# A hybrid decoder step on one Trainium2 core: layer-norm scaling and weight subtracts from GpSimd to VectorE, second buffers for loaded rows, squares out of PSUM, first combinations in product order

## The chip, the cores and the metric

The kernel runs on one core of one Trainium2 chip. It is written with a tile framework: tiles come from pools with a number of buffers, and a scheduler puts the instructions into one queue for each engine. The metric is the device time of one execution in microseconds (us); lower is better. Before the change three runs gave 3063.54, 3064.39 and 3066.76 us, median 3064.39.

The engines are named as in the profile: PE is TensorE (matmuls), PEld its weight loads, DVE is VectorE, ACT is ScalarE, POOL is GpSimd, SP is SyncE, which here issues most of the DMAs. Each engine works off its own queue in order; an instruction that waits holds up all that stand behind it.

## The reference

One step of a two-layer decoder on 1024 prompt rows and 64 sample rows of width 1024, in float32. Layer 0 mixes with a gated short convolution, layer 1 with differential attention (prompt rows causally, sample rows against a paged cache of 2048 keys). After each mixer comes a SwiGLU feed-forward net of width 2816, and after each of the four parts a layer norm over the residual sum.

```python
# layer 0:
gb, gc, h = split(x @ w_in, 3);  u = gc * h
conv = w_taps[0]*u_pad[:, 0:S] + w_taps[1]*u_pad[:, 1:S+1] + w_taps[2]*u_pad[:, 2:S+2]
m = (gb * conv) @ w_out
# layer 1: q, k, v = rope(split(x @ w_qkv, 3)); a = softmax(q1 k1) - lam * softmax(q2 k2)
#          m = (rmsnorm(a @ v) * subln_g * (1 - lam_init)) @ w_attn_out
# both layers:
x = layernorm(ALPHA * x + m) * ln_mix_g + ln_mix_b
x = layernorm(ALPHA * x + (silu(x @ w_gate) * (x @ w_up)) @ w_down) * ln_ffn_g + ln_ffn_b
```

Beside the two `x` (1024 and 64 rows) the outputs are the convolution's last rows and the new keys and values.

## The kernel before

**Precision.** A float32 operand is split in two parts: `hi` is a rounded copy made by ScalarE, `lo` the rest, made by a subtraction (`split_to`, lines 78 to 80). A product is then three matmuls, hi x hi, hi x lo and lo x hi (`passes`). So each loaded tile costs one cast on ScalarE (L79) and one subtract (L80 on VectorE, or L91 on GpSimd in two halves).

**Stages, in order of time.** Loading of `x` and the first combinations (0 to 47 us); the convolution's in-product (to 292); its out-product (to 457); FFN0 in (to 955) and out (to 1304); attention (1304 to 2061); its out-product (2073 to 2238); FFN1 in (to 2717) and out (to the end).

**In-products** (`InPhase`) are Strassen products with seven instead of eight block products. The seven combinations of the blocks of `x` are held split in `xh` and `xl` (`Combos`); those of the weights, `ws`, are made step by step from loaded `raw` tiles by `Weights.make`. The names B11, B21, B22, X1 to X4 are the combinations; the first products need them in the order B11, B21, X3, X2, X1, X4, B22. PE's order is written out by hand there. `load_x` makes the first set of combinations: for two halves `ch` of the columns and two halves `kk` of the inner index it loads four blocks, and makes all seven combinations of one `kk` before it goes to the next.

**Out-products** (`OutPhase`) take row tiles of 128 in three groups (`PAIRED` = (0,4,1), (5,2,6), (3,7) for conv and attention, `PLAIN` = (0,1,2), (3,4,5), (6,7) for the FFNs). For each group they run over all steps `f` (8 in conv and attention, 22 in the FFNs). A step needs a weight tile (`raw`, split to `whi` and `wlo`) and the rows (`hr` from DRAM, split to `hh` and `hl`), and in the first group the sample rows `hs`. `prep` issues them three steps ahead. `whi` and `wlo` come from a pool of seven buffers (`wsp`, tag "w"), `hh` and `hl` from two, `hr` and `hs` from one. Two tiles of a group use 6 matmuls each in a step. At the end of a group `ln_prompt` does the layer norm of each tile: residual sum on VectorE (L416), square with row sum on ScalarE (L421, whose unused full output goes over the product's PSUM tile), the rest on VectorE and GpSimd. Turning the rows into the next stage's operand (transposes on PE, casts and subtracts) goes into the following group's steps, as the list `side`. In the FFN stages the residual rows `x` are first multiplied with the gain and added to the bias of the layer norm before (L374, L375 on GpSimd), since the rows were stored without these.

**What sets the order.** Outside blocks marked `manual_schedule` the framework's scheduler sets the order of each engine's queue, from dependencies, buffers and its own idea of durations. So a buffer more, or work on another engine, can change the order of instructions that aren't touched. In PE's case the in-products and the attention are in the written order.

Lines the text speaks of: L79 (casts), L80 and L91 (subtracts), L222 (a weight combination), L260 (in-products), L345 (out-products), L385 (sample rows' product), L416 to L431 (layer norm), L835 (sample rows' q, k, v in attention), L1048 (prompt rows' q, k, v), L1158 to L1176 (the last normalisation in attention and its transposes).

## Time and profile before

| | |
|---|---|
| three runs | 3063.54, 3064.39, 3066.76 us |
| the profiled execution | 3066.03 us, span 3064.3 us |
| PE busy | 2787.6 us, 91% of the span |
| VectorE busy | 1490.7 us, 49% |
| ScalarE busy | 1095.6 us, 36% |
| GpSimd busy | 506.7 us, 17% |
| granted PE clock, mean | 0.969 |

The profile is of one execution. Busy times of matmuls overlap a little, since they are pipelined. A row of groups reads: line, engine, operation, output <- inputs (partitions x elements), count, busy us, mean ns of one, idle of that engine just before and what ended it. A wait is put down to what came last by the profile. The granted clock is PE's, 1.00 at full speed.

### The profile page before, as it was taken

The page shows a single profiled execution, that of the slowest core. Times are in us where ns is not written, and L with a number is a line of the kernel's source. Part 1 is how long each engine was busy: PE and PEld are TensorE (multiplying, and loading weights), DVE is VectorE, ACT ScalarE, POOL GpSimd, SP SyncE. Part 2 cuts the span into 40 slices and gives each one's busy share as a digit, 9 for nine tenths or more (in the row PEclk, how much of TensorE's full clock was granted, in tenths as well). Part 3 has the DMA queues.
Part 4 walks back from the last instruction along what each step waited for, and adds up shares of the span by engine and source line. Part 5 has one row for each costly group of instructions (what it writes and reads, how often), then busy time and mean ns, then how long its engine had stood idle before and what let it go on. Part 6 is the DMA issues. An engine that isn't in the chain of part 4 may idle for free. (4 is left out here: it accounts for less than half of the span.)

```text
span 3064.3 us, 51378 instructions
## 1 busy us (share of the span) xinstructions
PE 2787.6 (91%) x20468; PEld 2372.9 (77%) x20468; DVE 1490.7 (49%) x2527; ACT 1095.6 (36%) x2080; POOL 506.7 (17%) x638
## 2 busy tenths in 40 slices
PE   5999869999998988689999999988789999989886
PEld 5999559999995666479888666655579999976664
DVE  6675355445443365322222566662565454543553
ACT  4322364333331233211221556552553333322332
POOL 1001550000002031011111232344410000020310
PEclk8999999999999999989999999998899999999999
DMA  3222542222224455366787888735422222244653
GB/s 109 69 73 70 179 155 78 79 78 71 81 79 142 135 180 185 127 222 217 247 282 263 292 301 305 262 105 163 154 88 77 78 71 85 77 134 141 200 180 110
DMA packets 193442, 455.45 MB, mean 149 GB/s; under 512 B 43025, under 2 KB 84514, under 8 KB 193202
## 3 DMA queue, kind: packets, MB, share of 16 engines
q1 hardware_dynamic: 180322, 408.05, 40.6%
q0 software_dynamic: 12160, 42.81, 4.1%
q8 instruction: 160, 2.62, 0.4%
q10 hardware_dynamic: 720, 1.31, 0.1%
q14 instruction: 80, 0.66, 0.1%
HBM read 387.66 MB, written 64.43 MB: 148 GB/s over the span
## 5 line engine op out<-in xcount | busy, mean ns | idle before, releaser
L260 PE MATMUL pin<-xh,ws 128*128 128x272 f32 x6272 | 1204.6, 290 | 46.2 <-ACT gc L284 12.4
L260 PEld LDWEIGHTS pin<-xh,ws 128*128 128x128 f32 x6272 | 1001.2, 190 | 52.8 <-ACT gc L284 12.9
L260 PE MATMUL pin<-xl,ws 128*128 128x272 f32 x3136 | 913.1, 291 | 8.0 <-DVE xl L80 8.0
L260 PEld LDWEIGHTS pin<-xl,ws 128*128 128x128 f32 x3136 | 594.7, 190 | 9.4 <-DVE xl L80 9.1
L345 PE MATMUL pout<-whi,hh 128*128 128x512 f32 x960 | 408.1, 426 | 109.6 <-ACT hh L79 106.0
L345 PE MATMUL pout<-whi,hl 128*128 128x512 f32 x960 | 389.6, 417 | 30.9 <-DVE hl L80 30.6
L345 PE MATMUL pout<-wlo,hh 128*128 128x512 f32 x960 | 392.9, 410 | 7.1 <-DVE wlo L80 7.1
L80 DVE TENSOR_TENSOR wlo<-raw,whi 128x1024 fp32r<-128x1024 f32 x156 | 211.5, 1357 | 337.5 <-ACT whi L79 163.1
L345 PEld LDWEIGHTS pout<-whi,hh 128*128 128x128 f32 x960 | 189.8, 198 | 216.7 <-ACT hh L79 156.6
L79 ACT CAST whi<-raw 128x1024 fp32r<-128x1024 f32 x156 | 163.5, 1048 | 405.5 <-DMA raw<-wfo 197.3
L79 ACT CAST ws<-s 128x512 fp32r<-128x512 f32 x224 | 139.0, 622 | 442.9 <-PE pin L260 415.2
L80 DVE TENSOR_TENSOR ws<-s,ws 128x512 fp32r<-128x512 f32 x212 | 146.3, 690 | 262.8 <-ACT ws L79 262.8
L345 PEld LDWEIGHTS pout<-whi,hl 128*128 128x128 f32 x960 | 190.8, 199 | 96.2 <-DVE hl L80 55.0
L345 PEld LDWEIGHTS pout<-wlo,hh 128*128 128x128 f32 x960 | 190.8, 199 | 51.7 <-DVE wlo L80 9.2
L1048 PE MATMUL psqkv<-whi,xTh 128*128 128x256 f32 x768 | 223.1, 290 | 5.6 <-ACT pout L421 5.6
L80 DVE TENSOR_TENSOR hl<-hr,hh 128x384 fp32r<-128x384 f32 (+1 forms) x180 | 125.5, 697 | 205.6 <-ACT hh L79 187.9
L1048 PE MATMUL psqkv<-wlo,xTh 128*128 128x256 f32 x768 | 214.8, 280 | 0.0
L1048 PE MATMUL psqkv<-whi,xTl 128*128 128x256 f32 x768 | 214.5, 279 | 0.0
L374 POOL TENSOR_TENSOR x<-x,lng 128x1024 f32<-128x1024 f32 x16 | 41.9, 2621 | 1032.5 <-DMA x<-x_dram 995.6
L79 ACT CAST ws<-raw 128x512 fp32r<-128x512 f32 x168 | 104.2, 621 | 294.9 <-PE pin L260 203.5
L1048 PEld LDWEIGHTS psqkv<-whi,xTh 128*128 128x128 f32 x768 | 145.3, 189 | 21.6 <-issue 14.5
L91 POOL TENSOR_TENSOR wlo<-raw,whi 128x512 fp32r<-128x512 f32 x96 | 131.5, 1392 | 153.5 <-ACT whi L89 95.7
(224 smaller groups left out, 3587.4 us busy)
## 6 DMA issues: line engine op xcount, KB each, us to landing
raw<-wfo SPq DMA_DIRECT2D x132, 512.0 KB, 3.6
kpg<-ck SPq DMA_DIRECT2D x128, 512.0 KB, 5.2
vpg<-cv SPq DMA_DIRECT2D x128, 512.0 KB, 5.0
raw<-wfi SPq DMA_DIRECT2D x88, 512.0 KB, 3.8
h_dram<-ev SPq DMA_DIRECT2D x88, 272.0 KB, 3.1
raw<-wco SPq DMA_DIRECT2D x24, 512.0 KB, 4.0
x_dram<-x SPq DMA_DIRECT2D x24, 512.0 KB, 2.6
x<-x_dram SPq DMA_DIRECT2D x24, 512.0 KB, 4.4
```

Source lines behind the costliest of these rows:

```text
L79: ACT.copy(hi, src)
L80: (eng or DVE).tensor_tensor(lo, src, fv(hi), op=ALU.subtract)
L91: POOL.tensor_tensor(lo[:, cs], raw[:, cs], fv(hi[:, cs]), op=ALU.subtract)
L260: PE.matmul(ps[:, c, :CW], a, y, start=(start and k == 0 and m == 0), stop=(k == 3 and m == 2), skip_group_check=True)
L345: PE.matmul(ps[:, hf, :], a, b, start=(f == 0 and m == 0), stop=(f == self.nf - 1 and m == 2))
L374: POOL.tensor_tensor(kept[t], kept[t], gb[ln["n"] - 1][0], op=ALU.mult)
L1048: PE.matmul(ps[t][:, t % 2, :256], a[:, k, t0:t0 + P], b_[:, cs], start=(k == 0 and n == 0), stop=(k == KT - 1 and n == 2), skip_group_che ...
```

## The change

It does six things.

1. The weight subtracts of the conv and attention out-products (`wlo`, formerly two halves on GpSimd) and those of the first weights of the conv and of each FFN (`ws`) run on VectorE.
2. The multiply and add on the residual rows in the FFN out-products move from GpSimd, at a group's start, to VectorE, one instruction a step from step 8 on.
3. `hr` and `hs` get two buffers.
4. The square of the layer norm writes its unused output to a BF16 tile `junk` in SBUF, not over the PSUM tile.
5. `load_x` makes each combination for both `kk` before the next combination, in the products' order, and asks for a weight after each.
6. The pool of FFN0's out stage lies on the right side of SBUF.

```diff
@@ load_split
-        if sub is POOL:
-            ACT.copy(hi, raw)
-            for cs in (slice(0, width // 2), slice(width // 2, width)):
-                POOL.tensor_tensor(lo[:, cs], raw[:, cs], fv(hi[:, cs]), op=ALU.subtract)
-        else:
-            split_to(hi, lo, raw, sub)
+        split_to(hi, lo, raw, sub)
@@ OutPhase.prep
-                raw = hp.tile(shape, F32, name="hr", tag="hr", bufs=1)
+                raw = hp.tile(shape, F32, name="hr", tag="hr", bufs=2)
...
-                    hs = hp.tile([P, 2, 32], F32, name="hs", tag="hs", bufs=1)
+                    hs = hp.tile([P, 2, 32], F32, name="hs", tag="hs", bufs=2)
@@ OutPhase.run
+            ln["junk"] = lambda: pool.tile([P, D], BF16, name="junk", tag="junk", bufs=1)
...
-                    if gb:
-                        POOL.tensor_tensor(kept[t], kept[t], gb[ln["n"] - 1][0], op=ALU.mult)
-                        POOL.tensor_tensor(kept[t], kept[t], gb[ln["n"] - 1][1], op=ALU.add)
...
+                    if gb and 8 <= f < 8 + 2 * len(ts):
+                        x = kept[ts[f // 2 - 4]]
+                        DVE.tensor_tensor(x, x, gb[ln["n"] - 1][f % 2], op=(ALU.mult, ALU.add)[f % 2])
@@ ln_prompt
-        ACT.activation(ps.rearrange("p a b -> p (a b)"), x, AF.Square, bias=nmu[:, 0:1], accum_out=ss)
+        if gb is None:
+            junk = scp.tile([P, D], BF16, name="junk", tag="sc")
+        else:
+            junk = ln["junk"]()
+        ACT.activation(junk, x, AF.Square, bias=nmu[:, 0:1], accum_out=ss)
@@ load_x (the blocks are now made and loaded for both kk, in the order k, t, then kk)
-                            def put(n, x, sub=None):
+                        def put(n, src):
+                            for kk in range(2):
                                 ks = slice(2 * kk, 2 * kk + 2)
-                                split_to(xc.h[:, n, ks, cs], xc.l[:, n, ks, cs], x, sub)
+                                split_to(xc.h[:, n, ks, cs], xc.l[:, n, ks, cs], blk[kk][src[0]][:, src[1]])
+                            if ch == 0:
+                                conv.prep(len(conv.made) + 1)
...
+                        def less(dst, a, b):
+                            for kk in range(2):
+                                d, x, y = (blk[kk][k][:, t] for k, t in (dst, a, b))
+                                DVE.tensor_tensor(d, x, y, op=ALU.subtract)
...
+                        put(B11, b11)
+                        put(B21, b21)
+                        less(b11, b12, b11)
+                        less(b12, b22, b12)
+                        put(X3, b12)
+                        less(b12, b22, b11)
+                        put(X2, b12)
+                        put(X1, b11)
+                        less(b21, b21, b12)
+                        put(X4, b21)
+                        put(B22, b22)
@@ callers
-            self.into = InPhase(xc, [(Weights(..., sub=POOL if f == 0 else None), Put(f)) for f in range(FT)])
+            self.into = InPhase(xc, [(Weights(...), Put(f)) for f in range(FT)])
-                                             *((ACT, POOL) if not work else ())), put))
+                                             *((ACT,) if not work else ())), put))
-                out = OutPhase(KT, z_dram, i_["wco"], PAIRED, POOL)
+                out = OutPhase(KT, z_dram, i_["wco"], PAIRED)
-        with tc.tile_pool(name="fo0", bufs=2, reuse_waits="tile") as pool:
+        with tc.tile_pool(name="fo0", bufs=2, side="right", reuse_waits="tile") as pool:
-        wao = OutPhase(KT, a_dram, i_["wao"], PAIRED, POOL)
+        wao = OutPhase(KT, a_dram, i_["wao"], PAIRED)
```

The scheduler's order of the queues changes with it. ScalarE in the last group of FFN1's out stage, before; the tiles are the weight casts of steps 10, 11 and 12 and the row casts of steps 7, 8 and 9:

```order
L79 CAST whi_30963<-raw_30961 128x1024
L79 CAST hh_30897<-hr_30895 128x256
L79 CAST whi_30987<-raw_30985 128x1024
L79 CAST hh_30921<-hr_30919 128x256
L79 CAST whi_31011<-raw_31009 128x1024
L79 CAST hh_30945<-hr_30943 128x256
```

And after the change, weight casts of steps 16, 17 and 18 and row casts of 15, 16 and 17:

```order
L79 CAST whi_31089<-raw_31087 128x1024
L79 CAST hh_31071<-hr_31069 128x256
L79 CAST whi_31113<-raw_31111 128x1024
L79 CAST hh_31095<-hr_31093 128x256
L79 CAST whi_31137<-raw_31135 128x1024
L79 CAST hh_31119<-hr_31117 128x256
```

The row cast stood behind the weight cast of three steps later, and now stands behind that of the next step.

GpSimd at the end of attention, where the out-product's first weights are prepared, before:

```order
L1158 COPY osr<-prl 128x1 x2
L91 TENSOR_TENSOR wlo<-raw,whi 128x512 x2
L1162 TENSOR_SCALAR prs<-osr 128x4
L1163 TENSOR_TENSOR prs<-prs,mhalf 128x4
L1164 TENSOR_TENSOR prs<-prs,osr 128x4
L1166 TENSOR_SCALAR ost<-ost,prs 128x128 x4
L1176 DMA a_dram_136<-oT 128x512
L91 TENSOR_TENSOR wlo<-raw,whi 128x512 x2
```

And after:

```order
L1161 COPY osr<-prl 128x1 x2
L1179 DMA a_dram_136<-oT 128x512
L1165 TENSOR_SCALAR prs<-osr 128x4
L1166 TENSOR_TENSOR prs<-prs,mhalf 128x4
L1167 TENSOR_TENSOR prs<-prs,osr 128x4
L1169 TENSOR_SCALAR ost<-ost,prs 128x128 x4
L1179 DMA a_dram_136<-oT 128x512
```

The two weight subtracts ahead of the small chain `prs` to `ost` have left the queue.

VectorE at the start, before (`xl` are parts of combinations, `xb` the differences between blocks):

```order
L80 TENSOR_TENSOR xl<-xb,xh 128x2x272 x2
L605 TENSOR_TENSOR xb<-xb 128x544
L80 TENSOR_TENSOR xl<-xb,xh 128x2x272
L606 TENSOR_TENSOR xb<-xb 128x544
L80 TENSOR_TENSOR xl<-xb,xh 128x2x272
L609 TENSOR_TENSOR xb<-xb 128x544
L80 TENSOR_TENSOR xl<-xb,xh 128x2x272
L612 TENSOR_TENSOR xb<-xb 128x544
```

And after:

```order
L80 TENSOR_TENSOR xl<-xb,xh 128x2x272 x2
L80 TENSOR_TENSOR ws<-raw,ws 128x512
L80 TENSOR_TENSOR xl<-xb,xh 128x2x272 x2
L80 TENSOR_TENSOR ws<-raw,ws 128x512
L80 TENSOR_TENSOR ws<-s_227,ws 128x512
L206 TENSOR_TENSOR s_242<-s_241,raw 128x512
L80 TENSOR_TENSOR xl<-xb,xh 128x2x272
L605 TENSOR_TENSOR xb<-xb 128x544
L80 TENSOR_TENSOR ws<-s_242,ws 128x512
L605 TENSOR_TENSOR xb<-xb 128x544 x3
```

Both halves `kk` of a combination now follow one another, and the weights' low parts `ws` stand between them on VectorE.

More of the change, by code (lines that the diff above doesn't have):

```diff
@@ L546, in last @@
                     self.store(1)
[L548 to L549 removed]
+            self.into = InPhase(xc, [(Weights(i_["wfi"][layer, 2 * f], i_["wfi"][layer, 2 * f + 1]), Put(f)) for f in range(FT)])
             self.out = OutPhase(FT, h_dram[layer], i_["wfo"][layer], PLAIN)
```

29 lines of the change are left out of this document (6 added, 23 removed).

## The prediction

> **What bounds the kernel now.** I read the busy shares first, then the windows by stage, then PE's waits, then single steps.
>
> ```profile
> PE 2787.6 (91%) x20468; PEld 2372.9 (77%) x20468; DVE 1490.7 (49%) x2527; ACT 1095.6 (36%) x2080; POOL 506.7 (17%) x638
> ```
>
> PE is busy for 91% of the span of 3064.3 us. No gain is larger than the 276.7 us in which PE stands, plus what PE loses by running at a lower clock. The windows show where. Columns: from and to, length, then busy us and instructions of PE, PEld, DVE, ACT, POOL, the granted clock, the DMA share, GB/s.
>
> ```profile
> 0.00:46.70 46.70, 13.84 (x61) 12.44 (x61) 38.02 (x51) 23.28 (x39) 11.66 (x14) 0.84 0.57 155
> 60.00:291.60 231.60, 229.91 (x1824) 229.35 (x1823) 152.68 (x271) 69.70 (x118) 18.10 (x28) 1.00 0.21 70
> 291.60:346.00 54.40, 49.43 (x226) 33.75 (x224) 15.07 (x24) 10.98 (x15) 19.53 (x15) 1.00 0.50 154
> 346.00:457.00 111.00, 76.92 (x332) 57.35 (x328) 65.03 (x106) 65.19 (x133) 61.63 (x54) 0.93 0.51 161
> 955.00:1073.00 118.00, 107.37 (x420) 68.58 (x418) 46.48 (x47) 29.53 (x40) 17.78 (x7) 0.95 0.42 127
> 1073.00:1191.00 118.00, 103.73 (x439) 80.38 (x438) 66.15 (x80) 43.29 (x63) 24.86 (x17) 0.96 0.58 180
> 1191.00:1304.40 113.40, 74.35 (x288) 51.67 (x287) 58.16 (x77) 40.08 (x60) 18.87 (x16) 0.94 0.44 145
> 2073.00:2119.00 46.00, 43.71 (x172) 28.62 (x172) 7.19 (x14) 9.53 (x13) 16.99 (x14) 0.97 0.52 163
> 2119.00:2238.50 119.50, 87.48 (x333) 65.63 (x332) 64.79 (x108) 65.63 (x133) 59.74 (x54) 0.83 0.47 150
> 2718.00:2843.00 125.00, 118.03 (x467) 75.78 (x466) 47.56 (x47) 31.09 (x42) 21.14 (x8) 0.95 0.52 163
> 2843.00:2953.00 110.00, 99.89 (x417) 78.37 (x416) 58.68 (x74) 40.63 (x55) 27.97 (x17) 0.95 0.63 195
> 2953.00:3053.00 100.00, 70.00 (x265) 48.05 (x263) 47.97 (x60) 30.50 (x46) 14.03 (x8) 0.95 0.41 138
> ```
>
> In the product stages (60:291.6 is one) PE is the bound, and this change has nothing to win there. It can win in the first 47 us and in the four output stages, where the groups of row tiles follow one another: conv out (291.6 to 457), FFN0 out (955 to 1304.4), attention out (2073 to 2238.5), FFN1 out (2718 to 3053). As the floor of a window I take PE busy times granted clock, its work at full clock: 346:457 has 76.92 x 0.93 = 71.5, 2119:2238.5 has 72.6.
>
> PE's waits, as PE's tile and line, what ended them, total us, count, mean:
>
> ```profile
> PE pout L345 <- ACT hh L79: 106.0, 82, 4.4
> PE pout L345 <- DVE hl L80: 30.6, 29, 3.9
> PE pin L260 <- ACT pout L421: 11.1, 2, 5.5
> PE psq L835 <- DMA raws<-wqkv: 7.0, 2, 6.9
> PE psoT L1172 <- POOL ost L1166: 6.7, 1, 6.7
> PE psqkv L1048 <- ACT pout L421: 5.6, 1, 5.6
> ```
>
> Most of it is one wait: the products wait for the cast of the rows, `hh`, on ScalarE. One step of FFN1's last group shows why (start, us, engine, instruction, idle before):
>
> ```profile
> 2988.70 1.04 ACT L79 CAST whi<-raw 128x1024 fp32r<-128x1024 f32 x1 [3.13 <-PE pout L345]
> 2989.65 0.40 ACT L79 CAST hh<-hr 128x256 fp32r<-128x256 f32 x1
> 2990.11 0.51 PE L345 MATMUL pout<-whi,hh 128*128 128x512 f32 x1 [1.44 <-ACT hh L79]
> 2992.76 0.40 PE L345 MATMUL pout<-whi,hl 128*128 128x512 f32 x1
> 2994.59 0.50 PE L345 MATMUL pout<-whi,hh 128*128 128x512 f32 x1 [1.44 <-ACT hh L79]
> ```
>
> `hh` is ready to run early, but stands on ScalarE behind a weight cast three steps ahead, which had idled 3.13 us for PE to free a weight buffer. So PE ends a step, ScalarE does 1.04 + 0.40, and PE stands for 1.44. This is a wait made by queue order, not by work.
>
> **The change part by part.** The sum is made against the profiled run, 3066.03 us (span 3064.3); the median is 3064.39, 1.6 lower, so gains are taken off the median.
>
> *Two buffers for rows, last groups (FFN).* The new order puts `hh` of step f behind the weight cast of f+1, no longer of f+3. That weight buffer is free early, and `hh` is done while PE is in the step before. The step then costs its 12 matmuls. From 2990.11 to 2992.76 lie 11 intervals, 0.24 each. In the middle group, where the wait is hidden for a while, six steps of 18 matmuls show the pace without it:
>
> ```profile
> 1161.03 0.52 ACT L79 CAST hh<-hr 128x384 fp32r<-128x384 f32 x1 [2.53 <-DMA hr<-h_dram]
> 1184.25 0.51 ACT L79 CAST hh<-hr 128x384 fp32r<-128x384 f32 x1 [0.41 <-DMA hr<-h_dram]
> ```
>
> 23.22 us for six steps is 3.87 a step, 0.215 a matmul. Between 0.24 and 0.215 I take 0.23: 12 x 0.23 = 2.77 against 2994.59 - 2990.11 = 4.48, so 1.71 a step. 13 steps of FFN1 and 14 of FFN0 run like this: 46. The idle of the two windows (39.1 + 30.0) less 27 x 1.44 leaves 30 at the groups' starts; I take a quarter, 8. Together 54, bounds 38 (only the 1.44, 27 times, less a little) and 77 (both windows at their floors, 69.9 and 66.5). After this, `hl` on VectorE is what comes late next.
>
> *Middle groups (FFN).* Here `hh` waits for the DMA of `hr`, which with one buffer can only start when `hl` of the step before is done: the two rows above show 2.53 and 0.41. Floors are 99.6 and 94.9, so 18.4 + 15.1 = 33.5 is to be had. The second buffer acts on just this, so I take three quarters: 25, bounds 12 and 33.
>
> *First groups (FFN).* Floors 102.0 and 112.1, so 16.0 + 12.9 = 29 to be had. The sample rows `hs` get two buffers as well, but PE's own work there is longer, and less stands: I take half, 14, bounds 5 and 29.
>
> *Multiply and add of `x` from GpSimd to VectorE (FFN), 16 instructions of 128x1024 in each stage.*
>
> ```profile
> L80 DVE TENSOR_TENSOR wlo<-raw,whi 128x1024 fp32r<-128x1024 f32 x67 | 94.2, 1408 | 148.8 <-ACT whi L79 90.0 <-PE pout L345 50.9 <-PE pouts L385 4.3
> L80 DVE TENSOR_TENSOR wlo<-raw,whi 128x1024 fp32r<-128x1024 f32 x13 | 15.9, 1225 | 31.9 <-PE pout L345 29.3 <-issue 2.6
> L80 DVE TENSOR_TENSOR hl<-hr,hh 128x256 fp32r<-128x256 f32 x12 | 5.1, 425 | 5.3 <-ACT hh L79 5.3
> ```
>
> The first row is FFN0's whole out stage, the others FFN1's last group, where GpSimd is nearly idle: the same subtract takes 1408 beside GpSimd and 1225 alone. So 16 x 1.23 = 19.7 is added to VectorE in each stage, and 67 x 0.18 = 12 and some for `hl` come off. VectorE is busy 46 of 118 in a first group, which hides it: 0. Without that cover it costs up to 19.7 a stage.
>
> *Weight subtracts from GpSimd to VectorE (conv out, attention out).* Groups of 346:457:
>
> ```profile
> L91 POOL TENSOR_TENSOR wlo<-raw,whi 128x512 fp32r<-128x512 f32 x30 | 41.3, 1399 | 41.8 <-PE pout L345 18.7 <-ACT whi L89 18.5 <-issue 4.5
> L80 DVE TENSOR_TENSOR xl<-xb,xh 128x512 fp32r<-128x512 f32 x21 | 17.1, 826 | 9.0 <-ACT xh L79 8.9
> L80 DVE TENSOR_TENSOR hl<-hr,hh 128x384 fp32r<-128x384 f32 x8 | 7.5, 943 | 6.4 <-ACT hh L79 6.2
> L80 DVE TENSOR_TENSOR hl<-hr,hh 128x256 fp32r<-128x256 f32 x8 | 4.8, 599 | 7.1 <-ACT hh L79 7.1
> L148 DVE TENSOR_TENSOR xb<-xb 128x512 f32<-128x512 f32 x3 | 3.0, 994 | 0.5 <-ACT xb L136 0.3
> ```
>
> 30 halves, so 15 subtracts at 1.23, add 18.5 to VectorE; seven halves of the first FFN weights at 0.67 (an estimate: the 0.71 of 544 columns, quoted below, cut to 512) add 4.7. Off comes what GpSimd as a neighbour cost: `xl` 0.83 against 0.67 (21 times), `hl` 0.94 against 0.64 (the 425 ns for 256 columns, taken half as long again) and 0.60 against 0.43 (8 times each), `xb` 0.99 against 0.67 (three lines of three): 10 in all. What else VectorE runs there may bring it to 17; I take 14. VectorE: 65.0 - 14 + 18.5 + 4.7 = 74, PE 72, ScalarE 65. Three engines of some 70 that feed one another won't overlap wholly, and the layer norms' entries stay. I take half the way to 74: 18 and 23, together 41, bounds 10 and 86 (both floors). This holds the second `hr` buffer and the two `pin` waits (11.1), whose bank a square no longer occupies. Of the first groups' idle and clock (5.0 and 3.6) I take 6, bounds 3 and 8.
>
> *Load and first combinations.*
>
> ```profile
> 10.86 1.80 DVE L80 TENSOR_TENSOR xl<-xb,xh 128x544 fp32r<-128x544 f32 x1
> 16.65 0.71 DVE L80 TENSOR_TENSOR xl<-xb,xh 128x544 fp32r<-128x544 f32 x1
> 10.61 3.18 POOL L80 TENSOR_TENSOR ws<-raw,ws 128x512 fp32r<-128x512 f32 x2 [9.78 <-ACT ws L79]
> ```
>
> Now PE has done 61 products by 46.7. The new order makes the operands of the first products for both halves of k at once, and the weight halves leave GpSimd; counted along the new order I put about 79 more products before that time: 79 x 231.6/1824 = 10. The second half's loads now stand in SP's queue behind a weight and wait for tiles freed later: 4 off. Term 6, bounds 0 and 12. By the Trainium skill, "SBUF — State Buffer", section "Who interferes with whom", VectorE with two inputs from SBUF and a reading GpSimd exclude each other, and the loser stands for the other's whole instruction. The rows agree that VectorE suffers (1.80 for 0.71), not by a whole 1.59; by the rule all 11.66 us of GpSimd would come back and the sum would be 6 higher.
>
> *Attention's entry and end.* At the entry the `raws` wait (6.9) goes, since the stage's buffers no longer lie where the next ones must. Of the 5.6 of `psqkv` the square that leaves PSUM gives a little, and a copy that now stands behind late casts takes as little back: 7, bounds 3 and 12 (all of 7.0 + 5.6). At the end:
>
> ```profile
> 2063.28 2.81 POOL L91 TENSOR_TENSOR wlo<-raw,whi 128x512 fp32r<-128x512 f32 x2 [1.68 <-ACT whi L89]
> 2068.42 2.22 PE L1172 MATMUL psoT<-ident,ost 128*128 128x128 f32 x4 [6.65 <-POOL ost L1166]
> ```
>
> GpSimd does 2.81 us of weights ahead of the small chain that PE waits for. It goes: 3, bounds 2 and 6.
>
> Sum: 54 + 25 + 14 + 0 + 41 + 6 + 6 + 7 + 3 = 156. 3064.4 - 156 = 2908.
>
> **The rivals.** *A, only the queue order counts.* The last groups (54), entry (7) and end (3) are won; in the other groups another queue holds: SP issues row loads behind weight loads that wait for a weight buffer, so `hr` comes no earlier. For it: the DMA of `hr` ends the idle before `hh` in the middle group. Against: that idle shrinks as the run goes on, as a buffer would. 3064 - 64 = 3000.
>
> *B, PE-bound nearly everywhere.* All windows reach nine tenths of the way to their floors: 0.9 x (77 + 33.5 + 29 + 86.4 + 8.6 + 12 + 12.6 + 6.7) = 239, so 2825. For it: the steady steps at 3.87. Against: group starts and layer norms still have chains over three engines.
>
> *S, slower: VectorE takes the place that ScalarE had.* A weight subtract waiting for its late weight buffer stands on VectorE ahead of `hl`, as the weight cast did ahead of `hh`. Then the last FFN groups gain nothing (1.22 + 0.43 against 1.44), and conv out and attention out lose 24 x 1.23 = 29.5 each less 14 of relief, 31 for both: 3064 + 31 - 16 (load, entry, end) = 3079. It decides from where VectorE's work in a group reaches PE's. For it: 74 against 72 in those windows. Against: 49% over the whole run, and the hold over `hl` is broken by the same new order. The Trainium skill, "Perfetto Trace Analysis", section "Optimizing Scalar/DVE Operations", speaks on this side: where VectorE is saturated, work is given to others, even GpSimd, and this change does the reverse. In these rows VectorE is at 59% and 54%.
>
> **How the numbers follow.** My case 68%, A 15%, B 12%, S 5%. A measurement here tells about 0.2%, 6 us. My case's terms, which won't all fall on one side (their bounds add up to 73 and over 200), give about 2860 to 2960. For 8 in 10 the range goes a little to both sides, 2850 to 2975; outside remain most of A, part of B, and S. Faster: my case, A and B but for 2% of A where its terms fail too, 93%; same 2%; slower 5%.
>
> **What would show it.** In the last FFN groups steps of about 2.8 us, and PE's wait for `hh` down from 106.0 to under 30; the `hl` wait no larger than 30.6 by much. In 346:457 and 2119:2238.5 VectorE busy some 70 to 75, no GpSimd subtract, length near 93 and 96. `psoT`'s wait near 4, no `psq` wait of 6.9, about 140 products by 46.7. If the `hl` or `wlo` waits grow by as much as `hh` loses, S holds; if only the last groups shorten, A.

## The result and the profile after

The changed kernel takes 2871.17 us (median of four, 2868.58 to 2873.51) against 3063.97 us for the kernel before on the same chip: a ratio of 0.937, interval 0.9354 to 0.9386. That is 193 us less; forecast were 156, and 2908 us in a range of 2850 to 2975. The profiled execution took 2873.51 us, its span is 2871.7.

The page's busy shares:

```profile
PE 2734.8 (95%) x20468; PEld 2356.4 (82%) x20468; DVE 1503.3 (52%) x2628; ACT 1089.7 (38%) x2080; POOL 259.6 (9%) x489
```

PE does the same 20468 matmuls and is now busy for 95% of the span. GpSimd has half its work left. VectorE has 101 more instructions and only 12.6 us more to do: the work that was added came back almost whole, since its other instructions got shorter.

Where the time went is seen by cutting both traces at the same events: the last product of each group of row tiles, in first groups that of the sample rows; attention ends where the first out-product after it begins. All numbers are us. In profiles of kernels with the same load stage its end lies between 298.8 and 302.2, so differences of 3 us there mean nothing.

| stage | before | after | gain | the prediction's term |
|---|---|---|---|---|
| load and conv in | 302.0 | 302.2 | -0.2 | 6 |
| conv out, first group | 44.5 | 39.6 | 4.9 | with attention out 6 |
| conv out, rest | 104.7 | 80.5 | 24.2 | with attention out 41 |
| FFN0 in, rest | 485.4 | 483.9 | 1.5 | 0 |
| FFN0 out, first group | 136.6 | 123.7 | 12.9 | with FFN1 14 |
| FFN0 out, middle group | 117.8 | 100.4 | 17.4 | with FFN1 25 |
| FFN0 out, last group | 107.8 | 66.6 | 41.2 | with FFN1 54 |
| attention | 774.5 | 764.9 | 9.6 | 7 + 3 |
| attention out, first group | 46.9 | 45.6 | 1.3 | above |
| attention out, rest | 112.5 | 81.0 | 31.5 | above |
| FFN1 in, rest | 485.5 | 486.6 | -1.1 | 0 |
| FFN1 out, first group | 126.7 | 121.8 | 4.9 | above |
| FFN1 out, middle group | 108.3 | 95.6 | 12.7 | above |
| FFN1 out, last group | 99.2 | 67.4 | 31.8 | above |
| after the last product | 12.0 | 11.9 | 0.1 | 0 |

Some of PE's waits after (tile and line of PE, what ended them, total us, count, longest; the prediction called the last column a mean, which it is not):

```profile
PE pin L255 <- ACT gc L279: 20.2, 2, 19.7
PE pin L255 <- ACT ws L79: 14.3, 3, 9.6
PE pout L340 <- DVE wlo L80: 11.0, 8, 2.6
PE pout L340 <- ACT hh L79: 5.4, 6, 1.2
PE psoT L1175 <- POOL ost L1169: 5.4, 1, 5.4
PE psqkv L1051 <- DVE x L412: 4.5, 1, 4.5
PE pout L340 <- DVE hl L80: 3.7, 6, 1.6
```

The wait for `hh` went from 106.0 us to 5.4, and `hl` didn't take its place (30.6 to 3.7). `psq` is gone from the list. The largest wait is now a single one of 19.7 us, in the first 47 us, which the prediction didn't see. Of the wait for `ws`, 9.6 us are the very start, before the first weight is there.

Windows of the changed kernel (same columns as before):

```profile
0.00:46.70 46.70, 14.45 (x60) 13.07 (x60) 37.41 (x61) 23.36 (x38) 0.49 (x7) 0.71 0.58 155
341.70:422.20 80.50, 70.16 (x308) 53.54 (x306) 58.95 (x104) 55.73 (x116) 10.53 (x17) 0.94 0.66 208
1029.80:1130.20 100.40, 97.19 (x438) 79.22 (x438) 62.23 (x82) 41.02 (x60) 11.94 (x11) 0.98 0.66 209
1130.20:1196.80 66.60, 64.45 (x288) 51.15 (x287) 50.20 (x70) 35.35 (x55) 8.95 (x9) 1.00 0.70 228
2007.40:2088.40 81.00, 69.16 (x306) 53.48 (x307) 58.15 (x102) 55.93 (x116) 10.36 (x17) 0.94 0.65 207
2696.80:2792.40 95.60, 92.87 (x409) 75.31 (x410) 58.64 (x73) 37.28 (x53) 13.51 (x11) 1.00 0.69 219
2792.40:2859.80 67.40, 63.76 (x265) 49.66 (x263) 44.38 (x62) 31.16 (x47) 7.66 (x6) 0.97 0.62 201
```

In the FFN's middle and last groups PE is busy for 95 to 97% of the time. They come near the floors that the prediction had from busy time and granted clock: 100.4 and 95.6 in the middle groups (floors 99.6 and 94.9), and 67.4 in FFN1's last (66.5). FFN0's last, with 66.6, is 3.3 under its floor of 69.9. So busy time times clock is an estimate and no bound; the prediction's windows were also up to 5.5 us longer than the groups as they are cut here. In the load stage nothing moved: 60 matmuls in 46.7 us against 61 before (the prediction calls single matmuls products there), and the granted clock was 0.71 instead of 0.84.

One step and a little of FFN1's last group, ScalarE and some of PE:

```profile
2838.13 0.41 ACT L79 CAST hh<-hr 128x256 fp32r<-128x256 f32 x1 [1.52 <-DMA hr<-h_dram]
2838.45 1.04 ACT L79 CAST whi<-raw 128x1024 fp32r<-128x1024 f32 x1
2841.13 0.41 ACT L79 CAST hh<-hr 128x256 fp32r<-128x256 f32 x1 [1.64 <-DMA hr<-h_dram]
...
2838.37 0.39 PE L340 MATMUL pout<-whi,hh 128*128 128x512 f32 x1
2839.05 0.39 PE L340 MATMUL pout<-whi,hh 128*128 128x512 f32 x1
```

ScalarE now idles for a DMA and not for PE. PE runs without a stop: three matmuls in 0.68 us, 0.23 each, which is what the prediction took. A steady step of 12 takes 2.75 us instead of 4.48.

### The profile page after: what moved, and what is told of

Same layout as the page of the kernel before. It is cut to its first block, busy times and chain, and to the rows that moved or that the text cites. A ratio compares the mean times of both kernels' runs of the same rounds, so it can differ in the third digit from the quotient of the medians.

```text
span 2871.7 us, 51247 instructions
## 1 busy us (share of the span) xinstructions
PE 2734.8 (95%) x20468; PEld 2356.4 (82%) x20468; DVE 1503.3 (52%) x2628; ACT 1089.7 (38%) x2080; POOL 259.6 (9%) x489
## 4 chain that ended last, share of the span: by engine, by line
PE 61%; issue 23%; DMA 7%; DVE 5%; ACT 3%; POOL 1%; SPq 1%; DVEq 0%; POOLq 0%; ACTq 0%
PE pin L255 21%; PE pout L340 14%; PE psqkv L1051 10%; PE psS L1121 3%; PE psO L954 3%; PE pso L1156 2%; PE psS L896 2%; DMA raw<-wfo 2%; PE psaT L1149 1%; PE pouts L378 1%; DMA hr<-h_dram 1%; PE psq L838 1%; DVE xl L80 1%; ACT xb L131 1%; DMA raw<-wfi 1%
## 5 line engine op out<-in xcount | busy, mean ns | idle before, releaser
L80 DVE TENSOR_TENSOR wlo<-raw,whi 128x1024 fp32r<-128x1024 f32 x204 | 252.6, 1239 | 315.1 <-ACT whi L79 200.4
L340 PE MATMUL pout<-whi,hh 128*128 128x512 f32 x960 | 388.9, 407 | 9.0 <-ACT hh L79 5.4
L340 PE MATMUL pout<-wlo,hh 128*128 128x512 f32 x960 | 382.4, 399 | 11.0 <-DVE wlo L80 11.0
L340 PE MATMUL pout<-whi,hl 128*128 128x512 f32 x960 | 382.6, 402 | 3.9 <-DVE hl L80 3.7
L79 ACT CAST whi<-raw 128x1024 fp32r<-128x1024 f32 x204 | 214.1, 1049 | 320.8 <-DMA raw<-wfo 212.7
L80 DVE TENSOR_TENSOR ws<-s,ws 128x512 fp32r<-128x512 f32 x224 | 154.5, 690 | 263.1 <-ACT ws L79 263.1
L340 PEld LDWEIGHTS pout<-wlo,hh 128*128 128x128 f32 x960 | 183.0, 191 | 53.8 <-DVE wlo L80 15.4
L97 POOL TENSOR_SCALAR rs_t<-lss 128x1 f32<-128x1 f32 x32 | 17.5, 546 | 1666.1 <-ACT junk L421 1665.9
L80 DVE TENSOR_TENSOR ws<-raw,ws 128x512 fp32r<-128x512 f32 x168 | 116.1, 691 | 78.9 <-ACT ws L79 78.8
L79 ACT CAST hh<-hr 128x384 fp32r<-128x384 f32 (+1 forms) x180 | 85.9, 477 | 187.6 <-PE pout L340 124.4
```

The costliest lines, as they stand in the source:

```text
L79: ACT.copy(hi, src)
L80: (eng or DVE).tensor_tensor(lo, src, fv(hi), op=ALU.subtract)
L340: PE.matmul(ps[:, hf, :], a, b, start=(f == 0 and m == 0), stop=(f == self.nf - 1 and m == 2))
```

## The experiments

Two theories stood against each other for the output stages. **Theory 1**: the second buffer for the rows lets the scheduler put the row cast ahead of the late weight cast, and that is the gain. **The rival**: it is the work taken off GpSimd, which had slowed VectorE. A **theory 2** says that the rival holds for the convolution's and the attention's out-products alone. A **theory 3** on the load stage came out of the trace after.

Each run is compared with runs of the kernel before beside it on the same chip. The medians of one kernel differ by some us from one set of runs to another (the change has 2871.17 and 2866.16), so the ratios count.

| run | median us | ratio to before, interval |
|---|---|---|
| the change | 2871.17 | 0.937, 0.9354 to 0.9386 |
| e1: only the second buffers | 2925.54 | 0.9553, 0.9538 to 0.9569 |
| e2: change without them | 2989.51 | 0.9775, 0.9742 to 0.9807 |
| e3: change, weight subtracts on GpSimd | 2890.03 | 0.9446, 0.9428 to 0.9465 |
| e8: only the weight subtracts moved | 3038.87 | 0.9929, 0.9907 to 0.9951 |
| e6: change, scaling on GpSimd | 2879.28 | 0.9413, 0.9391 to 0.9435 |
| e7: change, FFN0's pool on the left | 2873.73 | 0.9387, 0.9366 to 0.9408 |
| e10: change, square into PSUM | 2873.81 | 0.9405, 0.9381 to 0.9429 |
| e9: change, old load order | 2864.15 | 0.9374, 0.935 to 0.9399 |
| e4: change, second half apart | 2860.39 | 0.934, 0.9322 to 0.9357 |
| e5: e4, second half later | 2861.76 | 0.9348, 0.9326 to 0.9371 |
| e11: e5, constants after it | 2863.88 | 0.9366, 0.9344 to 0.9387 |
| e12: the change again | 2866.16 | 0.9373, 0.935 to 0.9396 |

And the stages of the profiled runs that answer the questions, cut as above:

| stage | before | after | e1 | e2 | e3 | e6 | e8 |
|---|---|---|---|---|---|---|---|
| conv out, rest | 104.7 | 80.5 | 92.0 | 97.9 | 87.2 | 81.0 | 101.6 |
| attention out, rest | 112.5 | 81.0 | 93.3 | 91.3 | 88.1 | 80.5 | 98.0 |
| FFN0 out, all | 362.3 | 290.7 | 298.2 | 345.1 | 289.5 | 297.9 | 360.8 |
| FFN1 out, all | 334.2 | 284.8 | 295.4 | 325.0 | 285.3 | 290.4 | 335.5 |

### e1: only the second buffers

```diff
-                raw = hp.tile(shape, F32, name="hr", tag="hr", bufs=1)
+                raw = hp.tile(shape, F32, name="hr", tag="hr", bufs=2)
...
-                    hs = hp.tile([P, 2, 32], F32, name="hs", tag="hs", bufs=1)
+                    hs = hp.tile([P, 2, 32], F32, name="hs", tag="hs", bufs=2)
```

> The kernel before, and only the second buffers for hr and hs added; GpSimd keeps its subtracts and scalings, the square stays in PSUM. Theory 1 (the queue order that the second buffer gives is what counts in the output stages): the steps of the FFN's last groups fall from 4.48 to about 2.7, FFN0 out and FFN1 out together get 90 to 120 us shorter of the 121 that the whole change won there, the wait of PE for hh falls from 106 to under 30, and the time is 2930 to 2970. Rival (the work taken off GpSimd, and with it the slowing of VectorE, is what counts): hl on VectorE stays slow and becomes what PE waits for, the FFN stages win under 60, and the time is above 3000.

Measured: 2925.54 us, ratio 0.9553, so 137 us of the 193. The FFN out stages fell from 696.5 to 593.6, 103 of the 121 won there. PE's waits in e1:

```profile
PE pout L345 <- DVE hl L80: 22.3, 14, 6.2
PE pout L345 <- POOL wlo L91: 7.1, 7, 2.5
PE pout L345 <- ACT hh L79: 4.8, 7, 2.3
```

The wait for `hh` is gone (4.8) by two lines of code alone, with all of GpSimd's work in place, and the late steps of the FFN's last groups take 2.75 us. The rival falls for the FFN. But it isn't wholly wrong: `hl` still costs 22.3, and the change as a whole brought it to 3.7. The conv and attention rests gained 31.9 of their 55.7, more than the 10 to 25 expected, which is why the time came out under the expected range. The buffers of `hr` and of `hs` were not tried one by one.

### e2: the change without the second buffers

```diff
-                raw = hp.tile(shape, F32, name="hr", tag="hr", bufs=2)
+                raw = hp.tile(shape, F32, name="hr", tag="hr", bufs=1)
...
-                    hs = hp.tile([P, 2, 32], F32, name="hs", tag="hs", bufs=2)
+                    hs = hp.tile([P, 2, 32], F32, name="hs", tag="hs", bufs=1)
```

> The changed kernel, with one buffer each for hr and hs again. Theory 1: the row cast goes back behind a late weight cast, steps of the FFN's last groups back towards 4.5 us, 60 to 110 us lost, 2930 to 2980. Rival (work taken off GpSimd): at most 20 lost, under 2892.

Measured: 2989.51 us (one of four runs 3003.65), ratio 0.9775; 118 us more than the change in the medians, 124 by the ratios, even over the upper end of 110. The step of the kernel before is back to the hundredth, with the other five edits in place:

```profile
1229.27 1.04 ACT L79 CAST whi<-raw 128x1024 fp32r<-128x1024 f32 x1 [3.13 <-PE pout L340]
1230.22 0.40 ACT L79 CAST hh<-hr 128x256 fp32r<-128x256 f32 x1
1230.67 0.50 PE L340 MATMUL pout<-whi,hh 128*128 128x512 f32 x1 [1.44 <-ACT hh L79]
```

So theory 1 holds from both sides: the buffers are worth 137 alone and 118 to 124 on top of the rest.

### e3 and e8: the out-products' weight subtracts

e3 puts them back on GpSimd in the changed kernel, e8 moves only them in the kernel before:

```diff
 e3, in the change:
-                out = OutPhase(KT, z_dram, i_["wco"], PAIRED)
+                out = OutPhase(KT, z_dram, i_["wco"], PAIRED, POOL)
-        wao = OutPhase(KT, a_dram, i_["wao"], PAIRED)
+        wao = OutPhase(KT, a_dram, i_["wao"], PAIRED, POOL)
 (and load_split with its branch for GpSimd; e8 is the reverse in the kernel before)
```

> The changed kernel, with the weight subtracts of the convolution's and the attention's out-products on GpSimd in two halves again, as before. Theory 2 (in these two stages it is the subtracts' place that counts: GpSimd takes 2.8 us a weight and slows VectorE): hl 128x384 back from 0.71 to about 0.94 us, VectorE no less busy although it has 15 subtracts fewer, the two stages together 25 to 45 us longer, 2896 to 2916. Rival (the second row buffer did it there too): at most 10 longer, under 2882. At the end of attention some 2 to 3 us are lost by both.

> The kernel before, and only the weight subtracts of the convolution's and the attention's out-products moved to VectorE; one row buffer, all else as before. Theory 2 (GpSimd as a neighbour costs VectorE as much as it takes from it): VectorE is no busier in those windows (about 60 us), the two rests of 104.7 and 112.5 get 10 to 30 us shorter together, 3035 to 3054. Rival S of the prediction (VectorE takes the place that ScalarE had): they get longer, up to 31, 3065 to 3095. The FFN stages stay as they were by both.

Measured: e3 2890.03 us, ratio 0.9446, some 23 more than the change by the ratios. Its profiled execution, the fastest of four, is 12.3 longer in the span, and the two rests are 6.7 + 7.1 = 13.8 longer. The 2 to 3 us at the end of attention were not lost: `psoT` waits 3.9 us there, 5.4 in the change. VectorE is busy for 57.5 us in e3's first rest, with 19 instructions fewer than in the change, which has 58.95. e8 3038.87, ratio 0.9929, 21 less than before; the rests won 3.1 + 14.5. How this is split over the two is not settled, since the granted clock moved too (0.93 to 0.90 in the first, 0.83 to 0.91 in the second). e3 lies between its two theories, e8 within what theory 2 expected. The place of the subtracts is worth 14 to 18 in these stages, the second buffers 28 (change against e2) to 32 (e1), all of the change 56. Rival S of the prediction (slower) falls with e8: even with one row buffer the move made the kernel 0.7% faster.

Why the subtracts on VectorE cost so little is seen in the groups of that stage. The kernel before (346 to 452), then e8 (343.1 to 444.7), then e3 (342 to 428):

```profile
L80 DVE TENSOR_TENSOR xl<-scs,xh 128x128 fp32r<-128x128 f32 x4 | 5.2, 1346 | 0.1
```

```profile
L80 DVE TENSOR_TENSOR xl<-xb,xh 128x512 fp32r<-128x512 f32 x21 | 13.9, 687 | 4.1 <-ACT xh L79 4.1
L80 DVE TENSOR_TENSOR xl<-scs,xh 128x128 fp32r<-128x128 f32 x4 | 0.9, 286 | 0.0
```

```profile
L80 DVE TENSOR_TENSOR xl<-xb,xh 128x512 fp32r<-128x512 f32 x15 | 15.4, 1051 | 5.2 <-ACT xh L79 5.1
L80 DVE TENSOR_TENSOR hl<-hr,hh 128x384 fp32r<-128x384 f32 x7 | 8.2, 1173 | 6.3 <-ACT hh L79 5.9
```

Where no GpSimd subtract runs beside it, the subtract of 128x512 takes 0.69 us (e8). The 0.83 of the kernel before (in the prediction) and the 1.05 of e3 are means over those that met one, 5 of 21 and 7 of 15, and those that met none. The one of 128x384 takes 0.55 in e8 and 1.17 in e3; the 0.71 of the change still holds one of 1.65 beside GpSimd's work on the sample rows. The small one of 128x128 goes from 0.29 to 1.35. Its four instructions in the kernel before show what happens, VectorE above, GpSimd below (start, us):

```profile
368.70 5.15 DVE L80 TENSOR_TENSOR xl<-scs,xh 128x128 fp32r<-128x128 f32 x4
368.55 5.16 POOL L91 TENSOR_TENSOR wlo<-raw,whi 128x512 fp32r<-128x512 f32 x4 [4.83 <-ACT whi L89]
```

The two engines go in step: each small subtract ends 0.15 us after the GpSimd subtract beside which it began. Here the rule that the prediction weighed for the load stage is seen (the Trainium skill, "SBUF — State Buffer", "Who interferes with whom": the loser stands for the other's whole instruction), and the trace agrees: VectorE loses what is left of GpSimd's instruction, here 1.06 of some 1.30 us.

### e6: the multiply and add back on GpSimd

```diff
+                    if gb:
+                        POOL.tensor_tensor(kept[t], kept[t], gb[ln["n"] - 1][0], op=ALU.mult)
+                        POOL.tensor_tensor(kept[t], kept[t], gb[ln["n"] - 1][1], op=ALU.add)
...
-                    if gb and 8 <= f < 8 + 2 * len(ts):
-                        x = kept[ts[f // 2 - 4]]
-                        DVE.tensor_tensor(x, x, gb[ln["n"] - 1][f % 2], op=(ALU.mult, ALU.add)[f % 2])
```

> The changed kernel, with the multiply and add on the residual rows in the FFN out stages on GpSimd again, at the group's start. Theory (GpSimd's two big instructions a tile slow VectorE while they run, and the steps at a group's start are short of slack): FFN0 out and FFN1 out together 6 to 18 us longer than the 575.5 of the changed kernel, 2877 to 2889. Rival (the second row buffers give enough slack, so PE doesn't see it): within 3 us, 2868 to 2874.

Measured: 2879.28 us, ratio 0.9413; by the ratios 12 us more than the change. The FFN out stages are 588.3 instead of 575.5, 12.8 longer, so the rival falls. Of this 10.4 lie in the last two groups (72.6 and 71.8 instead of 66.6 and 67.4), most of it in one step of each (the fifth, 11.1 and 8.1 us instead of 4.1 and 2.75). PE's waits:

```profile
PE pout L340 <- DVE wlo L80: 14.7, 9, 2.6
PE pout L340 <- DVE hl L80: 9.8, 12, 2.0
```

In that step of FFN1 GpSimd multiplies and adds, and two VectorE subtracts that take 1.21 and 0.42 alone take 3.43 and 2.57; PE stands for the second:

```profile
2802.58 3.13 POOL L370 TENSOR_TENSOR x<-x,lng 128x1024 f32<-128x1024 f32 x1 [0.45 <-DMA x<-x_dram]
2805.79 3.22 POOL L371 TENSOR_TENSOR x<-x,lnb 128x1024 f32<-128x1024 f32 x1
2803.37 3.43 DVE L80 TENSOR_TENSOR wlo<-raw,whi 128x1024 fp32r<-128x1024 f32 x1
2806.73 2.57 DVE L80 TENSOR_TENSOR hl<-hr,hh 128x256 fp32r<-128x256 f32 x1
2809.35 0.80 PE L340 MATMUL pout<-whi,hl 128*128 128x512 f32 x1 [1.99 <-DVE hl L80]
```

The edit moves this work to another engine and from a group's start to its later steps at once; which of the two counts was not tried apart.

### e7 and e10: the pool's side and the square's place

```diff
 e7:
-        with tc.tile_pool(name="fo0", bufs=2, side="right", reuse_waits="tile") as pool:
+        with tc.tile_pool(name="fo0", bufs=2, reuse_waits="tile") as pool:
 e10:
-        if gb is None:
-            junk = scp.tile([P, D], BF16, name="junk", tag="sc")
-        else:
-            junk = ln["junk"]()
-        ACT.activation(junk, x, AF.Square, bias=nmu[:, 0:1], accum_out=ss)
+        ACT.activation(ps.rearrange("p a b -> p (a b)"), x, AF.Square, bias=nmu[:, 0:1], accum_out=ss)
```

> The changed kernel, with the pool of FFN0's out stage on the left side again. Theory (the entry to attention waited because its first buffers lay where that stage's rows were): PE's wait of 6.9 us for raws comes back, attention is 5 to 10 us longer than 764.9, 2876 to 2882. Rival (the square's place in PSUM was what delayed the entry): attention within 2 us, 2869 to 2874.

> The changed kernel, with the layer norm's square written over its PSUM tile again. Theory (a product bank held 1.1 us longer is felt only where a stage's first product waits for it, twice 5.5 us before): the rests of conv out and attention out with the first FFN products get 2 to 6 us longer together, 2872 to 2880. Rival (nothing waits for that bank any more): within 2 us, 2868 to 2874.

Measured: e7 2873.73 us, ratio 0.9387. The expected 2876 to 2882 did not show in the time, which is not to be told from the change's. The trace tells more: attention takes 773.7 instead of 764.9, and the wait that the change had removed is back,

```profile
PE psq L838 <- DMA raws<-wqkv: 6.9, 2, 6.7
```

e10 2873.81 us, ratio 0.9405 beside 0.9373 for the change on the same chip, 7.6 us more in the medians, with intervals that overlap. PE's waits in e10:

```profile
PE pin L255 <- ACT pout L417: 14.3, 2, 7.2
PE psqkv L1047 <- ACT pout L417: 7.3, 1, 7.3
```

Both waits end by the square, as before. Against the change's second profile (e12) the FFN in stages are 4.2 and 2.0 longer and attention 2.5; against its first profile it is 2.9, 0.8 and 0.9. With the rests added, the two seams of the expected 2 to 6 cost 4.8 or 3.3. So a square that holds a product bank is felt at the three seams where a stage's first products wait for it; the waits show it, the size (5 to 9 us in all) is hardly clear of the scatter, and the time bears it out only weakly.

### The load stage: e9, e4, e5, e11

What held PE for 19.7 us is read from the changed kernel's ScalarE and PE:

```profile
38.46 1.92 ACT L79 CAST xh<-xb 128x544 fp32r<-128x544 f32 x3 [1.90 <-DVE xb L605]
40.42 0.39 ACT L279 COPY gc<-pin 128x272 f32<-128x272 f32 x1
...
40.86 0.60 PE L255 MATMUL pin<-xh,ws 128*128 128x272 f32 x1 [19.68 <-ACT gc L279]
```

PE did the first three products of the first half of the columns, 36 matmuls, and stopped. The fourth goes into the first one's bank, which ScalarE must have copied out before, to a tile `gc` with the tag s0. The same tag holds a block of `x` of the second half of the columns until that block's combinations are made. So the copy comes only at 40.4 us. Theory 3 says that this buffer sets the stage, in whatever order the combinations are made; e9 tests it with the old order, and e4 by giving four blocks of the second half tiles of their own:

```diff
 e9: load_x as in the kernel before (all seven combinations of one kk, then of the other; conv.prep(7) after the first half)
 e4, in load_x, for the second half of the columns:
-    blocks (kk, k) in tags s0, s1, s2, s3
+    blocks (0, 0) in two "ev" tiles, (0, 1) in s2, (1, 0) in an "ev" and a "raw" tile, (1, 1) in s3
```

> The changed kernel, with the loading and first combinations in the old order (all seven of one half kk, then of the other). Theory 3 (PE can't begin its fourth product before ScalarE's copy into the tile of x, in either order): the in-product ends within 3 us of 302.2, the time is 2868 to 2876. Rival (the product order won something that VectorE's seven extra weight subtracts gave back): the in-product ends 5 to 9 later, 2876 to 2882.

> The changed kernel, but for the second half of the columns four of the eight loaded blocks get tiles of their own (three evacuation tiles that are still free, and one raw tile), so that the tiles s0 and s1, into which the first product is evacuated, are free once the first half is done. Theory 3 (the first 40 us are bound by this: PE stands 19.7 us until ScalarE can copy the first product into s0, which holds a block of x until then): the copy comes at about 25 instead of 40.4, PE's wait falls from 19.7 to 3 to 6, the in-product ends 10 to 17 us earlier, 2854 to 2861. Rival (VectorE's 44 instructions set the end of the stage): the waits move but the in-product ends where it did, 2868 to 2874.

Measured: e9 2864.15 us, ratio 0.9374 beside 0.9373 for the change on the same chip; the in-product ends at 297.0 against 300.4 there. Time and end came out under the expected ranges, and the rival's loss of 5 to 9 us is absent. The trace is not as theory 3 has it, though (two of PE's stops, ScalarE's copy, and the window):

```profile
23.00 0.82 PE L255 MATMUL pin<-xh,ws 128*128 128x272 f32 x2 [11.68 <-DVE ws L80]
34.32 0.38 ACT L279 COPY gc<-pin 128x272 f32<-128x272 f32 x1
34.76 0.60 PE L255 MATMUL pin<-xh,ws 128*128 128x272 f32 x1 [5.07 <-ACT gc L279]
0.00:46.70 46.70, 15.68 (x80) 14.60 (x81) 38.07 (x63) 22.82 (x39) 0.49 (x7) 0.94 0.56 156
```

PE's fourth product begins right after the copy here too, but with the old order the copy comes 6 us earlier, at 34.3. PE waits longest for a weight subtract, which stands on VectorE behind the combinations. By 46.7 us 80 matmuls are done, against 60 in the change and 61 in the kernel before. So the order does move the copy, and the product order won nothing: it may have given back what the weights had won by leaving GpSimd, but in the in-product's end that is 3 to 5 us, hardly clear of the scatter, and in the time nothing.

e4 2860.39 us, ratio 0.934; the in-product ends at 297.0 instead of 302.2. PE's stops there (start, us, then in brackets the idle before):

```profile
25.00 0.59 PE L255 MATMUL pin<-xh,ws 128*128 128x272 f32 x1 [4.39 <-ACT gc L279]
29.25 0.60 PE L255 MATMUL pin<-xh,ws 128*128 128x272 f32 x1 [1.16 <-ACT gc L279]
42.89 0.59 PE L255 MATMUL pin<-xh,ws 128*128 128x272 f32 x1 [10.55 <-DVE gc L283]
```

The copy came early, as theory 3 has it, and the 19.7 fell to 4.4. But two thirds of what was won went into a new wait of 10.55: an add on VectorE that frees the next bank, which stood behind the whole of the second half's subtracts. Only 5 of the expected 10 to 17 us came at the in-product's end; the time lies in the expected range, but medians of one kernel differ by as much. e5 writes the second half after the fifth product, so that the add goes ahead, and e11 also moves six small constant loads behind the blocks:

```diff
 e5, in InPhase.run, and load_x split in its two halves of the columns:
+                    if at in mid:
+                        mid[at]()
...
-                load_x()
+                load_x(0)
-                conv.run(psum, out.more, (), [out.fill(psum, n) for n in range(2)])
+                conv.run(psum, out.more, (), [out.fill(psum, n) for n in range(2)], {5: lambda: load_x(1)})
 e11: the constants at the end of load_x(1), not of load_x(0)
```

> The kernel of the run before (second half of the columns in tiles of its own), and the loading and combining of that half is written after the fifth product's evacuation, so that the scheduler puts the first evacuations on VectorE ahead of it; nothing is left out. In the run before PE stood 10.6 us from 32.3 on, behind an add that VectorE took only after all 44 instructions of the load. Theory 3 (order of the queues, ScalarE's and then VectorE's, held PE): that wait falls under 4, the in-product ends at 286 to 292 instead of 297, the time is 2849 to 2856. Rival (VectorE's sum of work): the in-product ends at 296 to 298, 2858 or more.

> The kernel with the second half of the columns apart and written after the fifth product, and the small constants loaded after that half instead of before; nothing is left out. If VectorE, which had no gap over 0.5 us from 24 to 46 us there, is the bound, the earlier loads bring nothing: in-product ends at 292 to 294, 2856 to 2863. If the loads held it, 288 to 291, 2851 to 2857. By both it is 8 to 20 us under the changed kernel beside it.

> The changed kernel itself, to compare the three others with on one chip: 2868 to 2875.

Measured: e5 2861.76 us, ratio 0.9348. The wait of 10.55 became 1.57 and 4.92, and 120 matmuls are done by 46.7:

```profile
32.84 0.39 PE L255 MATMUL pin<-xh,ws 128*128 128x272 f32 x1 [1.57 <-DVE gc L285]
44.05 0.57 PE L255 MATMUL pin<-xh,ws 128*128 128x272 f32 x1 [4.92 <-DVE gc L285]
0.00:46.70 46.70, 23.00 (x120) 21.20 (x121) 39.36 (x66) 24.35 (x42) 0.49 (x7) 0.84 0.55 156
```

The in-product ends at 293.0, between the two expectations. e11 has 2863.88 us and 294.8. In e5 VectorE has no gap over 0.5 us between 24 and 46 us, so with the queues in order its sum of work is probably the next bound, as the rival had it; no run takes work off it to show this. Earlier loads (e11) bring nothing. The expected times of these runs (2849 to 2856 for e5, and for e11 8 to 20 us under the change) were missed; e12, the change itself, came 2 us under its range.

Is one of these faster than the changed kernel? On one chip e11 has 0.9366 and the change (e12) 0.9373, 2.3 us in the medians (2859.54 to 2866.55 against 2859.23 to 2868.37). That is not told apart. e4's ratio of 0.934 is 0.003 under the change's first, taken at another time, with intervals that overlap by a hair. The load stage is shorter in the profiles of e4, e5 and e11, by 5 to 9 us against 302.2, but the in-product's end moves between 298.8 and 302.2 in the runs that didn't touch it. No version here is shown to beat the change.

## Why the prediction was right, and where it wasn't

The forecast of 2908 us was 37 us too high, within its range. The path it named for the output stages is what the runs show; several terms were too small, and one mechanism, in the load stage, was wrong.

**The last groups (54; measured 73.0, bounds 38 and 77).** In the steady steps the mechanism was right in each part: the order, the 1.44, the 0.23 a matmul. They went from 4.48 to 2.75 us, 27 times 1.73 or 47, against 46 in the sum. The step that failed is "I take a quarter" of the 30 us of idle at the groups' starts: some 26 came. There the row cast had waited for its DMA, as in the middle groups, and not behind a late weight. In FFN1 before:

```profile
2966.01 0.41 ACT L79 CAST hh<-hr 128x256 fp32r<-128x256 f32 x1 [3.09 <-DMA hr<-h_dram]
2974.09 0.40 ACT L79 CAST hh<-hr 128x256 fp32r<-128x256 f32 x1 [4.17 <-DMA hr<-h_dram]
```

PE's waits for `hh` and `hl` between 2953 and 2982, 7.8 us, have no counterpart after. e1 shows 64.5 of the 73.0 with the buffers alone (142.5 instead of 207.0). Most of what is left is the multiply and add, which stood on GpSimd at just these starts: putting it back costs 10.4 in these two groups (e6).

**The middle groups (25; measured 30.1).** Three quarters was a little low; with 100.4 and 95.6 they stand near their floors. Rival A's price, another queue that holds the rows, was not there.

**The first groups (14; measured 17.8)** came out a little over their price, within the bounds. **The multiply and add (0)**: the cost of 0 was right, since the added work was hidden on VectorE. But taking it from GpSimd was worth 12.8 (e6), which the sum had booked nowhere; the rows of the prediction with 1408 beside GpSimd and 1225 alone had pointed to it.

**Conv out and attention out (41; measured 55.7, bounds 10 and 86).** The step that failed is "half the way to 74". The 74 was counted for a window of 111 us; in the rest as it is cut here VectorE had 60.0 before, which makes it 69, and it is busy for 58.95 and 58.15 us in 80.5 and 81.0. The missing 10 went mostly to the neighbours: in conv out's first group VectorE has 25 instructions and 15.1 us instead of 18 and 9.9, in FFN0 in 383 and 249.7 instead of 373 and 243.7. The relief of 14 was well taken: by e8, where only the subtracts move, 60.0 us and 20.0 of subtracts became 64.6, so some 15 came off. The gain was 71% and 76% of the way to the PE floors, and about half of it the row buffers' (31.9 alone, 27.7 on top of the rest).

**First groups of these (6; measured 6.2)** and **attention (7 + 3; measured 9.6)** hold in sum, attention by luck in its parts. At the entry e7 shows the 6.9 as the pool's side, with 8.8 for the stage. At the end the wait went from 6.65 only to 5.4, and the term 3 for it is not borne out. e8, which takes the subtracts off GpSimd there, has 5.3, but e1, which leaves them, has 5.3 too; e3, which puts them back, has 3.9 in two waits, and e6, which doesn't, 6.9. What sets this wait stays open.

**Load (6; measured -0.2).** The mechanism was wrong. "I put about 79 more products before that time" counted along the written order and VectorE's work, and overlooked that the fourth product needs a tile in which a block of `x` still lies. The sign was there in PE's row at 37.55 of the kernel before, where 11.90 us of idle end by `gc`, and the prediction didn't ask what `gc` itself had waited for. And the new order, which was to bring 79 matmuls, brought none: with the old one (e9) 20 more are done by 46.7. The 6 us more that the prediction set beside its sum for GpSimd's 11.66 us can't be told from these runs: e9, with the old order and without GpSimd's part, ends the in-product 5.0 earlier than the kernel before, in one profile and near the scatter.

**The rivals.** A (3000) falls by the middle groups. B (2825) was nearer than A: the FFN's last two groups did come near their floors, but not conv out, attention out and the load. S falls by e8. The range held because it was wide enough, not because errors cancelled: the four large terms were too small, by 19, 15, 5 and 4, and only the load was much too large, by 6.

## What to carry to other kernels

When an engine's wait repeats with the same length in every step, look at what stands ahead of the late instruction in its own queue. Here two lines that give two small tiles a second buffer were worth 137 us, because they let a scheduler put a short cast ahead of one that waits, and let the rows' loads start earlier; a sum of work would have shown nothing. And ask of each wait on an evacuation what the evacuation itself waited for: its destination may be the buffer that holds up the stage. A new order of the work ahead of it then gains nothing as long as that buffer comes free no earlier.

A window's PE busy time times the granted clock told within some 5% what the middle and last groups of the FFN took once its queues were in order. In these groups the second buffers alone brought most of that distance (e1), where the prediction had put a part of it at a quarter.

## What the hardware showed that was not expected

A VectorE subtract that began while a GpSimd subtract was running ended a fixed time after that one had ended: 0.55 us for 128x512, 0.41 for 128x384, 0.28 for 128x256 and 0.15 for 128x128, in the conv out stage of the kernel before and of e3, but for one that met only the last 0.04 us. One of 128x128 that read PSUM for one of its inputs ran through in 0.29 us beside a GpSimd subtract (e3). Alone these take 0.69, 0.55, 0.42 and 0.29, so all but 0.14 us of the work came after the wait. So the price is what is left of the GpSimd instruction, up to a whole one of 1.40, whatever the size of VectorE's own: small instructions suffer most in proportion (0.29 to 1.35). It fits this that the change added only 12.6 us to VectorE's whole sum, where it took 247 us off GpSimd.

The granted clock differed between the runs in the load stage without a rule that could be read from these traces. Over the first 46.7 us it was 0.71 in the change, with one stop of 19.7 us, and 0.84 in the kernel before, with stops of 5.7 and 11.9. It was 0.84 in e5, whose stops after the first matmul are under 5 us, but 0.94 in e9, with one of 11.68. In the FFN's last groups it went from 0.94 and 0.95 to 1.00 and 0.97.
